# Sums of squares and reciprocal roots of the norms kept in PSUM banks

## The chip, the cores and the metric

The kernel runs on one core of one Trainium2 chip. The metric is the device time of one execution in microseconds (us), the median of several runs. A core has five engines that run side by side, each through its own list of instructions in order, with semaphores between them: PE (TensorE: matrix products into PSUM), DVE (VectorE), ACT (ScalarE), POOL (GpSimd) and SP (it issues transfers here). SBUF is the on-chip working memory, PSUM the accumulator memory of eight banks that PE writes and that DVE and ACT read and write.

## What is computed

One step of a two-layer transformer trunk over 640 tokens: 512 latent and 128 context tokens, width 1024, all in float32. In each layer: a norm with a modulation, an input projection, three attention branches with gates, an output projection, a second norm, a gated feed-forward part; one last norm at the end.

```python
def rmsnorm(x, g):
    xf = x.astype(jnp.float32)
    y = xf * lax.rsqrt(jnp.mean(xf * xf, axis=-1, keepdims=True) + EPS)
    return (y * g.astype(jnp.float32)).astype(x.dtype)

def trunk_layer(x, cvec, lp, mix_fn):
    sh1, sc1, g1, sh2, sc2, g2 = modulation(cvec, lp['w_mod'], lp['b_mod'])
    mixed, kv = mix_fn(rmsnorm(x, lp['norm1_g']) * (1.0 + sc1) + sh1)
    x = x + g1 * mixed
    x = x + g2 * swiglu(rmsnorm(x, lp['norm2_g']) * (1.0 + sc2) + sh2, lp['w_ffn_in'], lp['w_ffn_out'])
    return x, kv
```

## The kernel before

The state x lies transposed: eight tiles (`kt` or `m`, 0 to 7) of 128 channels by 640 tokens, each worked on in two halves of 320 tokens. A product of float32 precision is made of three passes with a high and a low part of each operand: `group` (lines 491 to 493) issues `wh·xh`, `wh·xl`, `wl·xh`. The low part of a weight tile, `wlo = raw - whi`, is made by POOL in one pass over 128x1024 (`lo`, line 457); in the attention part of the program some are made by an adding transfer instead.

A norm takes these steps, by half. `square_add` (lines 702 to 710), called as soon as a tile of x is final: ACT writes the square into an SBUF tile `sq`, DVE adds it to `ssq`. There is one `sq` buffer in the pool of line 1774 (two in the very first norm), so square and add of successive tiles take turns. When all eight are added, `rstd` (line 712) multiplies `ssq` by a matrix of ones on PE, into a PSUM bank of the kind `D`; ACT and DVE make the reciprocal root from it in four steps and leave it in the SBUF tile `ssq`. Then `norm` (line 731) goes through the eight tiles: DVE `nu = x * a * r` (line 749), ACT `h_hi = nu + b` (line 750), and for the low part either DVE `h_lo = (nu + b) - h_hi` (line 756) or, for tiles 2 and 5, ACT and POOL (lines 753 and 754). Each finished tile releases the matrix products that read it.

There are five norms: at the start; after the output projection of layer 0 (the second norm of layer 0, about 745 to 785 us); after its feed-forward part (the first norm of layer 1, about 1226 to 1260 us); after the output projection of layer 1 (its second norm, about 1929 to 1970 us); and the last one (about 2389 us to the end, `final`, line 1966). In the second norms the products `x2 = xr + g * d` are made from the bank `d` of the output projection by `residual` (line 1515), called in `out_proj` (line 1523); in the first norm of layer 1 and the last one by `ffn_out` (line 1729).

PSUM has four banks under the tag `B`, which the kinds `D` and `T` share, and four more for scores or, in the feed-forward part, under the tag `F`. There, two `D` banks and the four `F` banks go round as one list (`bank`, `bank_done`).

The order of the instructions on each engine is fixed when the program is built: `_Order` runs the tasks against a list of costs and priorities and writes the instructions down in the order in which they would start. DVE carries, beside the norms, the modulation of the layer (`mod_dve`, line 565, the rows `md`), and the small constants of the next attention (`attention_setup`, line 1932, the rows `lams` and `nlam`).

Of the kernel before, what the change touches and what calls it, by code (L numbers as in the profile page):

```python
# [26 lines left out]
AF = mybir.ActivationFunctionType  # L27
ALU = mybir.AluOpType
# [4 lines left out]
D = 1024  # L33
# [224 lines left out]
class _Trunk:  # L258
# [440 lines left out]

    def square_add(self, x, half, ssq, first):
        s = slice(half * HALF, (half + 1) * HALF)
        if first:
            yield self.act(ssq, x[:, s], AF.Square)
        else:
            q = yield from self.get("sq", [P, HALF])
            yield self.act(q, x[:, s], AF.Square)
            yield self.tt(ssq, ssq, q, ALU.add)
            self.rel("sq")  # L710

    def rstd(self, ssq):

        nc = self.nc
        d = yield from self.get("D", [P, 512])
        d = d[:, 0:HALF]
        yield self.pe(4 * HALF / 2400, lambda: nc.tensor.matmul(d, lhsT=self.ones, rhs=ssq, start=True, stop=True))
        u = yield from self.get("nu", [P, HALF])
        v = yield from self.get("nv", [P, HALF])
        yield self.act(u, d, AF.Ln, scale=1.0 / D, bias=self.eps)  # L720
        yield self.ts(v, d, 1.0 / D, EPS, ALU.mult, ALU.add)
        self.rel("D")
        yield self.act(ssq, u, AF.Exp, scale=-0.5)
        yield self.tt(u, ssq, ssq, ALU.mult)
        yield self.stt(u, u, -0.5, v, ALU.mult, ALU.mult)
        yield self.stt(ssq, u, 1.5, ssq, ALU.add, ALU.mult)
        self.rel("nu")
        self.rel("nv")
        return ssq

    def norm(self, l, which, x, half, ssq, h, ready, done):

        r = yield from self.rstd(ssq)
        left = [KT]

        def one(kt):
            yield self.wait(self.mod_ok[l][(0 if which == 0 else 12) + kt // 2])
            yield self.wait(self.mod_ok[l][(4 if which == 0 else 16) + kt // 2])
            a = self.acol[l][:, 8 * which + kt, :]
            sh = self.modc[l][:, (0 if which == 0 else 24) + kt, :]  # L740
            u = yield from self.get("nu", [P, HALF])
            o = half * HALF
            parts = []
            for s0, s1, c in self.segs(half):
                w = slice(s0 - o, s1 - o)
                b, hi = sh[:, c:c + 1], h[kt][:, 0, s0:s1]
                v = u[:, w]
                ops = [
                    self.stt(v, x[kt][:, s0:s1], a[:, c:c + 1], r[:, w], ALU.mult, ALU.mult),
                    self.act(hi, v, AF.Identity, bias=b),  # L750
                ]
                if kt in (POOL_FIRST if l == which == 0 else POOL_KT):
                    ops.append(self.act(v, v, AF.Identity, bias=b))
                    ops.append(self.ptt(h[kt][:, 1, s0:s1], v, hi.bitcast(F32), ALU.subtract))
                else:
                    ops.append(self.stt(h[kt][:, 1, s0:s1], v, b, hi.bitcast(F32), ALU.add, ALU.subtract))
                parts.append(ops)
            for ops in zip(*parts):
                yield self.both(*ops)
            self.rel("nu")  # L760
            self.o.fire(ready[kt])
            left[0] -= 1
            if left[0] == 0:
                self.rel("ssq")
                self.o.fire(done)

        for kt in range(KT):
            self.o.spawn(one(kt), 8 + half + 0.1 * kt)
# [754 lines left out]
    def out_proj(self, l, order, x2, ssq, ssq_ok):  # L1523
        src = self.I["x"] if l == 0 else self.xs
        hits = [self.counter(KT, lambda half=half: self.o.fire(ssq_ok[half])) for half in range(2)]
        ws, seen = {}, {m: 0 for m in range(KT)}
        xr, xr_ok = {}, {t: self.ev() for t in order}
        mg = self.merged
        first = [True, True]
        for m in range(KT):  # L1530
            x2[m] = self.t("x", [P, T])

        def load():
            for m, half in order:
                t = xr[m, half] = yield from self.get("xr", [P, HALF])
                yield self.dma(t, src[m][:, half * HALF:(half + 1) * HALF], 128 * 4 * HALF)
                self.o.fire(xr_ok[m, half])

        self.o.spawn(load(), 22)
        for m, half in order:  # L1540
            if m not in ws:
                ws[m] = yield from self.chunk()
            d = (yield from self.get("D", [P, 512]))[:, 0:HALF]
            yield from self.product(
                d, self.tiles(ws[m]), [lambda k=k: mg[k]["o"] for k in range(KT)], half,
                [mg[k]["half"][half] for k in range(KT)],
            )
            seen[m] += 1
            if seen[m] == 2:
                self.chunk_done()  # L1550

            def after(m=m, half=half, d=d, first_=first[half]):
                yield self.wait(xr_ok[m, half])
                for j in (8, 9, 10, 11):
                    yield self.wait(self.mod_ok[l][j])
                yield from self.residual(x2[m], xr[m, half], d, half, self.g1h[l][:, m, :])
                self.rel("D")
                self.rel("xr")
                if first_ and half == 0:
                    self.o.spawn(self.preload(), 8)  # L1560
                yield from self.square_add(x2[m], half, ssq[half], first_)
                hits[half]()

            first[half] = False
            self.o.spawn(after(), 7)
        for _ in range(KT):
            self.rel("u")
# [161 lines left out]
    def ffn_out(self, l, part, act, act_ok, x, ssq, ssq_ok, save):  # L1729

        end = part[-1] == NF - 1
        hits = [self.counter(KT, lambda half=half: self.o.fire(ssq_ok[half])) for half in range(2)]
        cur = {}
        n = len(part)

        def after(m, half, d):
            yield self.wait(self.mod_ok[l][20 + m // 2])
            xh = x[m][:, half * HALF:(half + 1) * HALF]
            yield from self.residual(x[m], xh, d, half, self.modc[l][:, 40 + m, :])
            self.bank_done(d)  # L1740
            if not end:
                return
            if m == half == 0:
                self.o.spawn(self.preload(), 8)
            yield from self.square_add(x[m], half, ssq[half], m == 0)
            hits[half]()
            if save and half == 1:
                yield self.dma(self.xs[m], x[m], 128 * 4 * T)

        split = (FO_SPLIT if end else KT) * n  # L1750
        steps = [(i // n, i % n, half) for i in range(split) for half in range(2)]
        steps += [(i // n, i % n, half) for half in range(2) for i in range(split, KT * n)]
        ds = {}
        for m, j, half in steps:
            if (m, half) not in ds:
                ds[m, half] = yield from self.bank()
            i, k = m * n + j, part[j]
            if i // 8 not in cur:
                cur[i // 8] = yield from self.chunk()
            wh, wl = (a[:, (i % 8) * P:(i % 8) * P + P] for a in cur[i // 8])  # L1760
            yield self.wait(act_ok[k])
            a, d = act[k], ds[m, half]
            yield self.group(d, wh, wl, a[:, 0, half], a[:, 1, half], j == 0, j == n - 1)
            if half == 1 and (i % 8 == 7 or i == KT * n - 1):
                self.chunk_done()
            if half == 1 and m == KT - 1:
                self.rel("act")
            if j == n - 1:
                self.o.spawn(after(m, half, d), 7)
# [463 lines left out]
```

## Time and profile before

| what | us |
|---|---|
| median of 3 runs | 2412.13 (2408.89 to 2419.16) |
| the profiled execution | 2411.09 |
| its span, first to last instruction | 2409.3 |
| PE busy | 2314.3 (96%) |
| DVE busy | 1771.2 (74%) |
| ACT busy | 1273.9 (53%) |
| POOL busy | 914.1 (38%) |

The profile is of one execution, with times from the start of its span. In its rows `L749` is a line of the kernel, though most operations are recorded by helpers and carry the helper's line: L336 is an activation of ACT, L359 and L363 are operations of DVE on two tensors, L375 one of POOL. `h<-nu,mo,h` says that h is written from nu, mo and h; `B`, `S` and `F` are PSUM banks, all other names stand for SBUF tiles or, on a transfer, for DRAM. "Idle before" is the time in which the engine had nothing running ahead of a row, and the name behind the arrow is what released it. The granted clock of PE is given as a share: 1.00 is 2.4 GHz, and it has one lower level, 1.2 GHz.

### The profile page before, as it was taken

What the parts mean: (1) busy time and instruction counts of PE and PEld (TensorE: products, weight loads), DVE (VectorE), ACT (ScalarE), POOL (GpSimd) and SP (SyncE); (2) the same over time, 40 slices, a digit from 0 to 9 for tenths busy, and PEclk for the clock granted to TensorE, in tenths of its full rate; (3) what the DMA queues carried; (4) which work ended last, traced back from release to release, by engine and by line L of the source; (5) the groups of instructions that cost most, each with busy time, mean ns of one, the idle gap of its engine ahead of it and who ended that gap; (6) DMA issues with size and microseconds to landing.
All of it is one profiled execution on the core that took longest, in us unless ns stands there. A gap on an engine that the chain in (4) does not pass through costs nothing.

```text
span 2409.3 us, 44479 instructions
## 1 busy us (share of the span) xinstructions
PE 2314.3 (96%) x16628; PEld 2265.0 (94%) x16628; DVE 1771.2 (74%) x4151; ACT 1273.9 (53%) x2818; POOL 914.1 (38%) x770
## 2 busy tenths in 40 slices
PE   7999899999998999999999999999999999999997
PEld 4999899999998999999889998999999989999997
DVE  7577788668489998999765778887672499666375
ACT  5677677667434432422457776777664254234143
POOL 3533411322123454645523425112221335456372
PEclk9999999999999999999989999999999999999998
DMA  6234332433774355453245444224436423322222
GB/s 252 75 94 115 77 85 59 108 88 88 207 233 151 107 164 172 135 171 128 95 135 123 99 111 98 72 64 101 107 85 145 133 100 114 106 71 85 74 76 74
DMA packets 100583, 275.79 MB, mean 114 GB/s; under 512 B 11408, under 2 KB 25360, under 8 KB 100368
## 3 DMA queue, kind: packets, MB, share of 16 engines
q1 hardware_dynamic: 84528, 215.28, 26.9%
q0 software_dynamic: 15840, 57.68, 12.5%
q8 instruction: 131, 2.15, 0.4%
q14 instruction: 84, 0.69, 0.1%
HBM read 208.43 MB, written 6.82 MB: 89 GB/s over the span
## 4 chain that ended last, share of the span: by engine, by line
PE 63%; DVE 13%; issue 7%; POOL 4%; DMA 3%; ACT 3%; DVEq 0%; POOLq 0%; SPq 0%; ACTq 0%
PE B L491 9%; PE B L492 8%; PE B L493 8%; PE F L493 6%; PE F L492 6%; PE F L491 5%; PE B L1127 4%; PE B L821 2%; PE B L823 2%; PE B L822 2%; PE S L1099 2%; POOL wlo L375 2%; PE S L1098 2%; PE B L1363 2%; PE B L1362 2%
## 5 line engine op out<-in xcount | busy, mean ns | idle before, releaser
L375 POOL TENSOR_TENSOR wlo<-raw,whi 128x1024 fp32r<-128x1024 f32 x158 | 391.9, 2486 | 350.5 <-ACT whi L336 340.4
L336 ACT ACTIVATE whi<-raw 128x1024 fp32r<-128x1024 f32 x268 | 282.9, 1055 | 257.7 <-PE F L492 89.7
L491 PE MATMUL B<-h,whi 128*128 128x320 f32 x972 | 308.2, 317 | 0.3 <-DVE acc L363 0.3
L493 PE MATMUL B<-h,wlo 128*128 128x320 f32 x972 | 301.0, 310 | 0.2 <-DMA wlo<-raw 0.2
L492 PE MATMUL B<-h,whi 128*128 128x320 f32 x972 | 300.6, 309 | 0.0
L821 PE MATMUL B<-whi,h 128*128 128x256 f32 x928 | 276.0, 297 | 1.8 <-ACT nat L336 1.2
L823 PE MATMUL B<-whi,h 128*128 128x256 f32 x928 | 264.6, 285 | 2.8 <-POOL h L375 2.5
L822 PE MATMUL B<-wlo,h 128*128 128x256 f32 x928 | 264.0, 284 | 0.0
L382 POOL DMA_DIRECT2D wlo<-raw x110 | 98.9, 899 | 323.9 <-ACT wlo L336 78.9
L336 ACT ACTIVATE P<-S,mx 128x768 f32<-128x768 f32 (+4 forms) x240 | 180.9, 756 | 54.6 <-DVE mx L1112 42.2
L491 PE MATMUL B<-u,whi 128*128 128x320 f32 x640 | 202.2, 316 | 0.4 <-DVE u L363 0.4
L375 POOL TENSOR_TENSOR wlo<-ws,whi 128x1024 fp32r<-128x1024 f32 x76 | 143.0, 1881 | 156.8 <-ACT whi L336 147.8
L493 PE MATMUL B<-u,wlo 128*128 128x320 f32 x640 | 198.3, 310 | 4.2 <-DMA wlo<-raw 4.2
L1112 DVE TENSOR_REDUCE mx<-S 128x1 f32<-128x768 f32 (+4 forms) x240 | 182.0, 765 | 22.7 <-PE S L1099 20.1
L492 PE MATMUL B<-u,whi 128*128 128x320 f32 x640 | 198.0, 309 | 0.0
L491 PEld LDWEIGHTS B<-h,whi 128*128 128x128 f32 x972 | 183.3, 189 | 1.3 <-DVE acc L363 0.6
L493 PEld LDWEIGHTS B<-h,wlo 128*128 128x128 f32 x972 | 182.9, 188 | 0.7 <-DMA wlo<-raw 0.7
L492 PEld LDWEIGHTS B<-h,whi 128*128 128x128 f32 x972 | 183.4, 189 | 0.0
L823 PEld LDWEIGHTS B<-whi,h 128*128 128x128 f32 x928 | 178.7, 193 | 3.9 <-POOL h L375 3.1
L821 PEld LDWEIGHTS B<-whi,h 128*128 128x128 f32 x928 | 179.0, 193 | 3.3 <-ACT nat L336 1.9
L822 PEld LDWEIGHTS B<-wlo,h 128*128 128x128 f32 x928 | 179.5, 193 | 0.0
L359 DVE TENSOR_TENSOR PT<-B,PT 128x512 fp32r<-128x512 f32 (+2 forms) x264 | 155.1, 608 | 32.5 <-ACT PT L336 30.5
(212 smaller groups left out, 7338.7 us busy)
## 6 DMA issues: line engine op xcount, KB each, us to landing
raw<-w SPq DMA_DIRECT2D x268, 512.0 KB, 3.4
wlo<-raw POOLq DMA_DIRECT2D x110, 512.0 KB, 4.7
mr<-wt SPq DMA_DIRECT2D x160, 256.0 KB, 3.2
u<-wm SPq DMA_DIRECT2D x12, 512.0 KB, 8.9
cr<-cb SPq DMA_DIRECT2D x14, 256.0 KB, 4.5
x<-x SPq DMA_DIRECT2D x8, 320.0 KB, 7.5
xr<-x SPq DMA_DIRECT2D x16, 160.0 KB, 3.5
xm<-x SPq DMA_DIRECT2D x8, 320.0 KB, 4.2
```

The source lines that it names most:

```text
L336: fn = lambda: self.nc.scalar.activation(out, in_, func, **kw)
L359: return self.dve(_n(out), lambda: self.nc.vector.tensor_tensor(out, a, b, op=op))
L375: return ("POOL", 0.147 + 0.0021 * _n(out), lambda: self.nc.gpsimd.tensor_tensor(out, a, b, op=op), 0.08)
L382: return ("POOL", 1.0, lambda: self.nc.gpsimd.dma_start(out=out, in_=in_, accum_op=ALU.add), 4.5)
L491: mm(out, lhsT=wh, rhs=xh, start=first, stop=False)
L492: mm(out, lhsT=wh, rhs=xl, start=False, stop=False)
L493: mm(out, lhsT=wl, rhs=xh, start=False, stop=last)
L821: mm(d, lhsT=hh, rhs=wh, start=kt == 0, stop=False)
L822: mm(d, lhsT=hh, rhs=wl, start=False, stop=False)
L823: mm(d, lhsT=hl, rhs=wh, start=False, stop=kt == KT - 1)
L1112: yield self.dve(w, lambda: nc.vector.tensor_reduce(m, s[:, 0:w], axis=AX.X, op=ALU.max, negate=True))
L1127: nc.tensor.transpose(t[:, i * P:(i + 1) * P], a, self.ident)
```

## The change

In the second norms of both layers, the first norm of layer 1 and the last norm, the square of a tile is written into the PSUM bank from which that tile of x was just made, and that bank is given back after the add and no more before the square. In the second norms and the first norm of layer 1, the reciprocal root is written over the product with ones in its PSUM bank, the eight `nu` products read it there, and the bank is given back after the eighth tile of the half. The first norm of layer 0 is as before; in the last norm the reciprocal root stays in SBUF.

```diff
-    def square_add(self, x, half, ssq, first):
+    def square_add(self, x, half, ssq, first, bank=None):
+
         s = slice(half * HALF, (half + 1) * HALF)
         if first:
             yield self.act(ssq, x[:, s], AF.Square)
+        elif bank is not None:
+            yield self.act(bank, x[:, s], AF.Square)
+            yield self.tt(ssq, ssq, bank, ALU.add)
         else:
...
-    def rstd(self, ssq):
+    def rstd(self, ssq, stay=False):
...
-        self.rel("D")
+        if not stay:
+            self.rel("D")
...
-        yield self.stt(ssq, u, 1.5, ssq, ALU.add, ALU.mult)
+        r = d if stay else ssq
+        yield self.stt(r, u, 1.5, ssq, ALU.add, ALU.mult)
...
-        return ssq
+        return r
...
-        r = yield from self.rstd(ssq)
+        stay = l > 0 or which > 0
+        r = yield from self.rstd(ssq, stay)
...
                 self.rel("ssq")
+                if stay:
+                    self.rel("D")
                 self.o.fire(done)
...
-                self.rel("D")
                 self.rel("xr")
                 if first_ and half == 0:
                     self.o.spawn(self.preload(), 8)
-                yield from self.square_add(x2[m], half, ssq[half], first_)
+                yield from self.square_add(x2[m], half, ssq[half], first_, d)
+                self.rel("D")
                 hits[half]()
...
-            self.bank_done(d)
             if not end:
+                self.bank_done(d)
                 return
             if m == half == 0:
                 self.o.spawn(self.preload(), 8)
-            yield from self.square_add(x[m], half, ssq[half], m == 0)
+            yield from self.square_add(x[m], half, ssq[half], m == 0, d)
+            self.bank_done(d)
             hits[half]()
```

On PE and POOL the order of the instructions is the same as before; on DVE, ACT and SP a few rows move. The first place is on DVE in the second norm of layer 0, where the reciprocal root of half 0 is finished while the last tiles of half 1 come in (x is the state, ac and mo the modulation, xr the old state, the numbers tell buffers apart). Before:

```order
L363 SCALAR_TENSOR_TENSOR ssq_8598<-nu_10107,ssq_8598 128x320
L363 SCALAR_TENSOR_TENSOR x_9569<-B_10115,gh_90,xr_10001 128x192
L363 SCALAR_TENSOR_TENSOR x_9569<-B_10115,gh_90,xr_10001 128x128
L363 SCALAR_TENSOR_TENSOR nu_10163<-x_9564,ac_89,ssq_8598 128x320
L363 SCALAR_TENSOR_TENSOR nu_10164<-x_9565,ac_89,ssq_8598 128x320
L359 TENSOR_TENSOR ssq_8599<-ssq_8599,sq_10173 128x320
L363 SCALAR_TENSOR_TENSOR h_10090<-nu_10163,mo_88,h_10090 128x320
```

And with the change:

```order
L363 SCALAR_TENSOR_TENSOR B_10088<-nu_10097,ssq_8598 128x320
L363 SCALAR_TENSOR_TENSOR x_9569<-B_10105,gh_90,xr_9994 128x192
L363 SCALAR_TENSOR_TENSOR x_9569<-B_10105,gh_90,xr_9994 128x128
L363 SCALAR_TENSOR_TENSOR nu_10152<-x_9564,ac_89,B_10088 128x320
L363 SCALAR_TENSOR_TENSOR nu_10153<-x_9565,ac_89,B_10088 128x320
L359 TENSOR_TENSOR ssq_8599<-ssq_8599,B_10105 128x320
L363 SCALAR_TENSOR_TENSOR h_10080<-nu_10152,mo_88,h_10080 128x320
```

The rows stand in the same order; the root, the `nu` products and the adds now name a bank, and the rows `h<-nu,mo,h` still name two SBUF tensors. It is the same in the second norm of layer 1.

The second place is on DVE in the first norm of layer 1, behind the row that reads the product with ones of half 1. Before:

```order
L371 TENSOR_SCALAR nv_15083<-B_15072 128x320
L359 TENSOR_TENSOR nat_15074<-nat_15070 128x128
L1955 TENSOR_REDUCE lams_15054<-nat_15074 128x2
L363 SCALAR_TENSOR_TENSOR h_14987<-nu_15086,mo_92,h_14987 128x320
L359 TENSOR_TENSOR nu_15082<-ssq_10487 128x320
```

And with the change:

```order
L371 TENSOR_SCALAR nv_15050<-B_15041 128x320
L363 SCALAR_TENSOR_TENSOR h_14961<-nu_15054,mo_92,h_14961 128x320
L359 TENSOR_TENSOR nu_15049<-ssq_10473 128x320
L363 SCALAR_TENSOR_TENSOR nu_15074<-x_9568,ac_93,B_14966 128x320
L363 SCALAR_TENSOR_TENSOR nu_15049<-nu_15049,nv_15050 128x320
```

The two small rows of the attention's constants (`nat`, `lams`) have gone behind the half's last `nu` products, so that the `h` row stands two rows further ahead. On SP, ahead of this norm, the load of one weight tile has gone behind the first store of the state (`xm<-x`), and the loads of three tables of constants for the next attention (rope, sm, lam) behind the last one.

## Rows read from the trace of the kernel before

**Rows 1.** The page, its first part: busy time, share of the span, instructions.

```profile
PE 2314.3 (96%) x16628; PEld 2265.0 (94%) x16628; DVE 1771.2 (74%) x4151; ACT 1273.9 (53%) x2818; POOL 914.1 (38%) x770
```

**Rows 2.** Windows around three norms: length, busy time by engine, PE clock, transfers.

```profile
core 0: us, PE busy (x) PEld busy (x) DVE busy (x) ACT busy (x) POOL busy (x), PEclk, DMA share, GB/s
...
750.00:768.00 18.00, 12.84 (x81) 11.95 (x79) 18.00 (x30) 8.58 (x16) 10.95 (x5) 0.93 0.25 87
...
1230.00:1245.00 15.00, 9.31 (x34) 7.34 (x34) 14.82 (x35) 10.11 (x21) 3.25 (x4) 0.60 0.78 204
...
1930.00:1950.00 20.00, 16.62 (x102) 15.44 (x101) 18.59 (x29) 11.28 (x20) 9.62 (x6) 0.91 0.23 79
1950.00:1970.00 20.00, 18.82 (x110) 18.05 (x109) 17.19 (x41) 11.49 (x29) 6.19 (x5) 0.83 0.31 102
```

**Rows 3.** Waits of PE, 745 to 770 us: total us, times, longest.

```profile
PE F L492 <- POOL h L375: 2.7, 1, 2.7
PE B L717 <- DVE ssq L359: 2.5, 2, 1.9
```

**Rows 4.** Waits of PE, 1225 to 1248 us.

```profile
PE B L823 <- POOL h L375: 2.5, 2, 1.8
```

**Rows 5.** Waits of PE, 1930 to 1958 us.

```profile
PE F L492 <- DVE h L363: 2.9, 1, 2.9
PE B L717 <- DVE ssq L359: 1.2, 1, 1.2
```

**Rows 6.** Timeline of DVE, second norm of layer 0: start, us, row, rows merged.

```profile
757.13 1.00 DVE L363 SCALAR_TENSOR_TENSOR nu<-x,ac,ssq 128x320 f32<-128x320 f32 x2
...
759.84 0.67 DVE L363 SCALAR_TENSOR_TENSOR x<-B,gh,xr 128x192 f32<-128x192 f32 x2
760.43 2.53 DVE L363 SCALAR_TENSOR_TENSOR nu<-x,ac,ssq 128x320 f32<-128x320 f32 x2
...
764.89 3.11 DVE L363 SCALAR_TENSOR_TENSOR nu<-x,ac,ssq 128x320 f32<-128x320 f32 x2
```

**Rows 7.** Timeline of POOL, the same stretch.

```profile
759.76 2.39 POOL L375 TENSOR_TENSOR wlo<-raw,whi 128x1024 fp32r<-128x1024 f32 x1 [3.56 <-ACT whi L336]
...
765.02 2.63 POOL L375 TENSOR_TENSOR wlo<-raw,whi 128x1024 fp32r<-128x1024 f32 x1 [0.40 <-ACT whi L336]
```

**Rows 8.** Groups of DVE over the whole span: count, busy us, mean ns, idle before.

```profile
L359 DVE TENSOR_TENSOR F<-F,s 128x320 f32<-128x320 f32 x60 | 29.1, 492 | 2.1 <-ACT s L336 1.5
L363 DVE SCALAR_TENSOR_TENSOR x<-F,mo,x 128x320 f32<-128x320 f32 x30 | 16.5, 550 | 60.9 <-PE F L493 60.9
```

**Rows 9.** Groups of ACT, 700 to 800 us.

```profile
L336 ACT ACTIVATE sq<-x 128x320 f32<-128x320 f32 x14 | 6.6, 468 | 27.2 <-DVE x L363 24.7 <-DVE ma L359 2.4
...
L336 ACT ACTIVATE B<-cr 128x512 f32<-128x512 f32 x2 | 1.2, 589 | 0.0
```

**Rows 10.** Timeline of DVE, second norm of layer 1.

```profile
1935.89 0.48 DVE L359 TENSOR_TENSOR ssq<-ssq,sq 128x320 f32<-128x320 f32 x1
...
1938.27 3.16 DVE L363 SCALAR_TENSOR_TENSOR nu<-x,ac,ssq 128x320 f32<-128x320 f32 x2
...
1941.75 1.00 DVE L363 SCALAR_TENSOR_TENSOR h<-nu,mo,h 128x320 fp32r<-128x320 f32 x2
...
1943.26 3.60 DVE L363 SCALAR_TENSOR_TENSOR nu<-x,ac,ssq 128x320 f32<-128x320 f32 x3
...
1947.19 0.54 DVE L363 SCALAR_TENSOR_TENSOR h<-nu,mo,h 128x320 fp32r<-128x320 f32 x1
...
1950.26 2.39 DVE L359 TENSOR_TENSOR ssq<-ssq,sq 128x320 f32<-128x320 f32 x1 [0.39 <-ACT sq L336]
```

**Rows 11.** Timeline of POOL, the same stretch.

```profile
1938.47 2.61 POOL L375 TENSOR_TENSOR wlo<-raw,whi 128x1024 fp32r<-128x1024 f32 x1 [3.36 <-ACT whi L336]
1942.55 0.93 POOL L375 TENSOR_TENSOR h<-nu,h 128x320 fp32r<-128x320 f32 x1 [1.48 <-ACT nu L336]
1943.50 2.56 POOL L375 TENSOR_TENSOR wlo<-raw,whi 128x1024 fp32r<-128x1024 f32 x1
```

**Rows 12.** Timeline of DVE, first norm of layer 1.

```profile
1235.79 1.96 DVE L363 SCALAR_TENSOR_TENSOR h<-nu,mo,h 128x320 fp32r<-128x320 f32 x1
```

**Rows 13.** Instructions of line 491, 1895 to 1945 us: duration ns, first and last start.

```profile
L491 PE MATMUL F<-h,whi x5: 305/309/411, 1942.0 to 1944.5; 128*128 128x320 f32 x5
```

**Rows 14.** Timeline of SP's queue, 1200 to 1260 us.

```profile
1205.49 9.51 SPq L378 DMA_DIRECT2D xm<-x  x3
...
1231.15 0.33 SPq L378 DMA_DIRECT2D xm<-x  x1
```

## The prediction

> **What bounds the kernel now.** I read the page first. PE is busy for 2314.3 of the span's 2409.3 us [rows 1], so what a norm can give back is time in which PE stands still, or runs at its lower clock, around a norm. The windows come next: they show PE busy for 12.84 of 18 us in the second norm of layer 0 (call it A), for 9.31 of 15 in the first norm of layer 1 (B), for 16.62 of 20 and 18.82 of 20 in the second norm of layer 1 (C) [rows 2]. PE is thus idle for 5.16 + 5.69 + 3.38 + 1.18 = 15.4 us in the three. DVE is busy for 18.00 of 18 in A, 14.82 of 15 in B and 18.59 of 20 in C: there it is the engine that is behind. The waits of PE say the same: it waits for the low part `h` or for `ssq`, products of DVE or of POOL behind DVE [rows 3 to 5].
>
> The granted clock falls in the same stretches, to means of 0.93, 0.60, 0.91 and 0.83 [rows 2]. At a lower level of 0.50 the time at half clock is (1 − mean) · 2 · length: 2.5 us in A, 12.0 in B, 3.6 + 6.8 = 10.4 in C. PE does half the work there, so these cost at most 1.25, 6.0 and 5.2 us.
>
> The third view is DVE's timeline beside POOL's. In A a pair of `nu` products takes 1.00 us at 757.13, but 2.53 at 760.43 and 3.11 at 764.89 [rows 6]. Both slow pairs lie over a POOL pass that makes a `wlo` tile: 759.76 for 2.39, 765.02 for 2.63 [rows 7]. Inside the first of these passes, at 759.84, DVE reads a bank, one tensor in SBUF and a small column (`x<-B,gh,xr`) and takes 0.67 for two rows [rows 6], so it isn't slowed. I read this as: a DVE row with two large SBUF inputs stands until POOL's pass ends, and a row with one of its inputs in PSUM doesn't. C repeats it: pair 3.16, trio 3.60, one add 2.39 [rows 10], with passes at 1938.47 and 1943.50 [rows 11].
>
> **What the change does, term by term.** It turns two of the rows that stand into rows with one SBUF input: `nu<-x,ac,ssq` (now with the bank for `ssq`) and `ssq<-ssq,sq` (now with the bank for `sq`). The rows of `h` and the squaring of the root keep two SBUF inputs. So a wait taken off a `nu` row may come back at the next `h` row, and each term has a low end for that.
>
> A. The two pairs lose 2.53 − 1.00 = 1.53 and 3.11 − 1.00 = 2.11 [rows 6]. If the next `h` takes over each wait, nothing is gained; if none does, 3.64. The order puts one add, now free to run, between the pair and its `h`, so a part is kept: I take the middle, **1.8**, range 0 to 3.6.
>
> B. `h` at 1235.79 takes 1.96 [rows 12], against 0.54 for a free one [rows 10]: 1.4 lost. Its inputs don't change, but two small rows leave the place ahead of it, so it may start before what holds it up. I take half, **0.7**, range 0 to 1.4. PE's 2.5 us behind POOL's `h` [rows 4] may hide it, which is the low end.
>
> C. The chain here is worked in order. The pair at 1938.27 is free, but the `h` pair behind it must stand until the pass ends at 1938.47 + 2.61 = 1941.08; it began at 1941.75, so 0.67 is kept. The trio at 1943.26 would take some 1.5 instead of 3.60, so 2.1 more. Its `h` at 1947.19 could start near 1944.4. POOL's second pass would be in its way: but POOL's own `h` before that pass [rows 11] waits for an ACT row behind the same `nu` rows, and can start at 1941.08 instead of 1942.55, which puts the pass at about 1942.0 to 1944.6. The `h` then starts near 1944.6, 2.6 earlier, and PE's 2.9 us of waiting for that row [rows 5] shrinks to 0.3. Last, the add at 1950.26 loses 2.39 − 0.48 = 1.9, and PE's product with ones waits for it. Sum 2.6 + 1.9 = **4.5**. Low end: the second pass stays where it was, to 1946.06, so that `h` gains 1.13, and with 1.9 that is 3.0. High end: every wait goes, 2.16 + 2.1 + 1.9 = 6.2.
>
> Clock. Less idle time should keep some of the lower clock away. Nothing at B, where most idle stays; at A and C 1.25 + 5.2 = 6.4 is the most. I take **1.5**, about a quarter, as about half of their 9.7 us of idle goes, and not all of that need lift the clock; range 0 to 3, and the whole of it is a rival.
>
> What I cost at nothing: ACT's square into a bank, since a 512-wide row into a bank takes 589 ns and a 320-wide square into SBUF 468 [rows 9], so the bank shows no surcharge; bounds ±0.1 us on each, and only a few are last in a chain. DVE with a bank as an operand: `x<-F,mo,x` takes 550 ns, `F<-F,s` 492 [rows 8], beside 0.54 for `h` [rows 10] and 0.48 for an add [rows 10]; at most 0.01 each. The last norm: its adds change, its `nu` rows don't, ±0.5. On SP, the weight load that goes behind the first of three stores (issued from 1205.49) is displaced by one issue, and the tables go behind the store at 1231.15 [rows 14] for an attention that starts after the norm; both lie beside PE's products. If that cover failed, a few tenths of a us for the load, and a wait of the next attention's DVE rows for the tables. The longer hold of the banks is priced as a rival.
>
> **Sum.** 1.8 + 0.7 + 4.5 + 1.5 = 8.5 us. The sum is made against the profiled execution, 2411.1 (span 2409.3): 2402.6. That execution lies 1.0 below the median of the three runs, 2412.1, so the forecast for a median is between 2402.6 and 2403.6: I say **2403**. Ends of the parts: 0 + 0 + 3.0 + 0 = 3.0, and 3.6 + 1.4 + 6.2 + 3 = 14.2, so this case's own range is 2397 to 2409.
>
> By these rows a PSUM operand costs nothing. The Trainium skill, page "Perfetto Trace Analysis", section "Optimizing Scalar/DVE Operations", gives DVE about 60 ns of access time on SBUF and about 125 ns on PSUM. The rows just named don't show these 65 ns; by the page the sum would be some 2 us smaller (worked out below).
>
> **Rivals.**
> - *The wait only moves.* The next `h`, or the squaring of the root, inherits each wait. For it: those rows still have two SBUF inputs. Against it: the add at C has no `h` behind it, and the passes end while free rows still run. Gain 1.9 (that add) plus about 0.7 (the `h` pair at C): some 2409.5. Chance 0.14.
> - *All waits go and the clock holds.* 3.6 + 1.4 + 6.2 + 6.4 = 17.6, so 2393.5 to 2394.5. Against it: `h` rows under a pass, and B's idle time, which is most of the clock's loss and barely moves. Chance 0.12 for over 14.2.
> - *A bank is dearer to read or write.* Some 36 DVE rows of this kind lie one behind the other on the three paths (eight `nu`, a root and seven adds of the half that comes last, three norms, less those under other work). The most that rows allow is 550 ns for `x<-F,mo,x` [rows 8] against half of the free pair of `nu`, 0.50 [rows 6]: 36 · 0.05 = 1.8 us less gain, 2404.8. Against it: one `h` without a bank takes 0.54 too. Chance 0.05. By the figure of the Trainium skill's page "Perfetto Trace Analysis" the estimate would be 36 · 0.065 = 2.3 us.
> - *Slower: the output projection of C runs out of banks.* Of four banks one is held by the root for eight `nu` rows, and each product's bank is now kept through the square and the add. The last product of half 1 ends when PE goes to `F<-h,whi` at 1942.0 [rows 13] and has 24 matmuls (eight tiles, three passes) of 16.62 / 102 = 0.16 each [rows 2], 3.9 in all, so it starts near 1938.1. It needs the bank whose add is now the row at 1935.89, which ends at 1936.4 [rows 10]: 1.7 us to spare. It decides from the point where that add comes more than 1.7 us later, as when one more POOL pass (2.6) stands over the DVE rows ahead of it. Then PE stands for up to 2.9 at C and a few tenths at A, the clock falls for as much again (2.9), and the gains are lost: 2411.1 + 6 = about 2417. Against it: the change makes DVE earlier, not later, and at 1935.89 no long row is near. Chance 0.04.
> - *It doesn't do what it says.* The order shows banks in the rows, so 0.01.
>
> The forecast keeps 0.64.
>
> **How the numbers follow.** 2395 to 2410 takes in the forecast's range and the first rival; outside lie half of the second rival, the fourth and a rest of the first, about 0.15. Half a per cent of 2412.1, about what a measurement of this kernel can tell from no change, is 12.1: faster means under 2400.1. Of the forecast, whose middle is 8.5, some 0.15 lies beyond 12.1; with all of the second rival that is 0.27. Slower, over 2424.2, would take the bank rival at more than twice its price: 0.02. The rest, 0.71, is within.
>
> **What would show it.** In the profile after, pairs of `nu<-x,ac,B` at 1.0 us under POOL's passes, and adds `ssq<-ssq,B` at 0.5, would show the mechanism right; pairs at 2.5 to 3 would show it wrong. `h` rows of 2 us or more, starting earlier, would show the first rival. PE's idle time should fall from 5.2 to about 3.4 at A, and from 4.6 to well under 2 at C; the mean clock in C should rise above 0.91 and 0.83. A wait of PE for `ssq` or an ACT square inside the output projection, at a `B<-u,whi` row, would show the banks. The forecast is wrong if free rows only let POOL's passes or the next engine (ACT's `h`, the weights' `whi`) become late by as much.

## The result and the profile after

The changed kernel takes 2399.01 us (median of 7 runs, 2396.04 to 2405.32) beside 2414.66 of the kernel before, measured with it (7 runs): a ratio of 0.9941, with a 95% interval of 0.9928 to 0.9954. It is faster by 0.6%, some 14 us. The profiled execution has a span of 2394.3 us, 15.0 less than the one read before. That is the forecast's direction, and the time lies within its range of 2397 to 2409. The gain is larger than that makes it look: the range was made from a median of 2412.13, and the kernel before came out at 2414.66 when it was measured again, so a gain of 14 to 15 lies at or just beyond the upper end of the forecast's 3.0 to 14.2 us.

All kernels of this study have PE's matmuls in one and the same order, so the n-th matmul of one trace is the n-th of another, and the span can be cut at the same work in both. The stages here are cut at PE's matmuls 5300 (737.0 us in the trace before), 6000 (856.4), 8300 (1216.7), 8600 (1267.0), 13500 (1915.1), 14200 (2035.4) and 16500 (2374.5); a number is the time between their starts. The last column runs from matmul 16500 to the start of the last one, the product with ones of the last norm.

| us | A: second norm, layer 0 | feed-forward, layer 0 | B: first norm, layer 1 | C: second norm, layer 1 | feed-forward, layer 1 | end, to the last matmul |
|---|---|---|---|---|---|---|
| before | 119.40 | 360.31 | 50.34 | 120.28 | 339.10 | 23.01 |
| after | 112.56 | 359.90 | 48.19 | 114.45 | 339.18 | 22.10 |
| difference | -6.84 | -0.41 | -2.15 | -5.83 | +0.08 | -0.91 |

The gain lies where it was looked for. What is not in the table is small: up to matmul 5300 the changed kernel takes 0.4 less, between 8600 and 13500 it takes 0.9 more, and from the start of the last matmul to the end of the span 12.30 instead of 11.84, so that 0.45 is left of the last column's 0.91.

The windows of the changed kernel, over the work of the four windows in [rows 2] to within five matmuls (length; busy time of PE, PE's loads, DVE, ACT, POOL; granted clock; transfers):

```profile
749.35:761.80 12.45, 11.61 (x78) 11.09 (x77) 12.45 (x30) 8.28 (x16) 9.63 (x5) 1.00 0.36 126
1222.90:1236.35 13.45, 9.15 (x35) 7.41 (x36) 13.15 (x32) 9.79 (x21) 2.63 (x3) 0.62 0.83 187
1921.65:1938.50 16.85, 15.59 (x102) 14.78 (x101) 15.95 (x29) 10.80 (x20) 9.40 (x6) 1.00 0.26 93
1938.50:1955.25 16.75, 16.44 (x111) 16.01 (x110) 14.75 (x41) 11.26 (x29) 4.45 (x5) 1.00 0.40 123
```

Two things are to be seen. PE's idle time fell from 5.16 to 0.84 in A, from 5.69 to 4.30 in B and from 4.56 to 1.26 + 0.31 = 1.57 in C. And the granted clock, 0.93, 0.91 and 0.83 before, is 1.00 in A and C; in B it stayed low, 0.62 after 0.60.

What the clock is worth is read from the stages of the table, which hold the same matmuls in both traces. A, B and C, before:

```profile
736.98:856.38 119.40, 109.29 (x703) 106.67 (x702) 115.83 (x230) 55.27 (x102) 52.22 (x27) 0.94 0.36 119
1216.69:1267.03 50.34, 44.65 (x302) 42.52 (x301) 33.91 (x84) 32.64 (x78) 17.83 (x26) 0.86 0.46 124
1915.08:2035.37 120.29, 110.54 (x703) 108.03 (x701) 105.46 (x187) 52.69 (x98) 51.90 (x26) 0.93 0.32 108
```

and after:

```profile
736.62:849.18 112.56, 106.45 (x703) 104.75 (x701) 109.44 (x229) 54.60 (x102) 52.05 (x27) 0.97 0.37 126
1209.08:1257.27 48.19, 43.67 (x302) 41.50 (x301) 32.10 (x84) 32.04 (x78) 16.78 (x26) 0.89 0.50 131
1906.23:2020.68 114.45, 107.39 (x702) 105.49 (x701) 98.33 (x187) 52.07 (x98) 50.24 (x26) 0.97 0.34 113
```

PE's idle time (length less busy time) fell by 4.0, 1.2 and 2.7 us, and its busy time for the same matmuls by 2.8, 1.0 and 3.1: nearly half of the gain is the higher clock.

DVE's timeline of A after, beside [rows 6]:

```profile
749.52 0.48 DVE L359 TENSOR_TENSOR ssq<-ssq,B 128x320 f32<-128x320 f32 x1
749.92 1.87 DVE L359 TENSOR_TENSOR nu<-ssq 128x320 f32<-128x320 f32 x1
...
752.23 0.15 DVE L359 TENSOR_TENSOR mo<-ma,sm 128x4 f32<-128x4 f32 x1
...
756.88 0.99 DVE L363 SCALAR_TENSOR_TENSOR nu<-x,ac,B 128x320 f32<-128x320 f32 x2
...
760.29 0.99 DVE L363 SCALAR_TENSOR_TENSOR nu<-x,ac,B 128x320 f32<-128x320 f32 x2
761.21 0.47 DVE L359 TENSOR_TENSOR ssq<-ssq,B 128x320 f32<-128x320 f32 x1
...
762.07 2.11 DVE L363 SCALAR_TENSOR_TENSOR h<-nu,mo,h 128x320 fp32r<-128x320 f32 x2
```

and POOL's, beside [rows 7]:

```profile
756.00 2.42 POOL L375 TENSOR_TENSOR wlo<-raw,whi 128x1024 fp32r<-128x1024 f32 x1 [0.89 <-ACT whi L336]
...
760.37 2.40 POOL L375 TENSOR_TENSOR wlo<-raw,whi 128x1024 fp32r<-128x1024 f32 x1 [0.34 <-ACT whi L336]
```

Both pairs of `nu` that took 2.53 and 3.11 now take 0.99, and they lie over POOL's passes as before. The last row shows what is left: an `h` pair, which still has two SBUF inputs, takes 2.11 (it began in the second of these passes, which ends at 762.77). The squaring of the root (749.92, 1.87) has taken over most of the wait of the add ahead of it, which took 2.28 before. And one small row was not in my working: before, the row `mo<-ma,sm` of the modulation, 128x4, stood under a pass too.

```profile
750.72 2.28 DVE L359 TENSOR_TENSOR ssq<-ssq,sq 128x320 f32<-128x320 f32 x1
...
753.85 2.37 DVE L359 TENSOR_TENSOR mo<-ma,sm 128x4 f32<-128x4 f32 x1
```

With the change it runs at 752.23 in 0.15, because DVE reaches it just before a pass (which starts at 752.48) instead of just behind the start of one (753.68 before): 2.2 us that come from a small shift. In C, DVE's timeline and then POOL's, beside [rows 10, 11]:

```profile
1929.40 1.00 DVE L363 SCALAR_TENSOR_TENSOR nu<-x,ac,B 128x320 f32<-128x320 f32 x2
...
1930.72 2.74 DVE L363 SCALAR_TENSOR_TENSOR h<-nu,mo,h 128x320 fp32r<-128x320 f32 x2
...
1933.96 1.45 DVE L363 SCALAR_TENSOR_TENSOR nu<-x,ac,B 128x320 f32<-128x320 f32 x3
...
1938.76 0.49 DVE L359 TENSOR_TENSOR ssq<-ssq,B 128x320 f32<-128x320 f32 x1 [0.40 <-ACT B L336]
```

```profile
1929.61 2.42 POOL L375 TENSOR_TENSOR wlo<-raw,whi 128x1024 fp32r<-128x1024 f32 x1 [3.36 <-ACT whi L336]
1931.98 1.13 POOL L375 TENSOR_TENSOR h<-nu,h 128x320 fp32r<-128x320 f32 x1
1933.07 2.64 POOL L375 TENSOR_TENSOR wlo<-raw,whi 128x1024 fp32r<-128x1024 f32 x1
```

The chain is the one that was worked out: the pair, the trio and the add are free (1.00, 1.45, 0.49 for 3.16, 3.60, 2.39), the `h` pair stands, and POOL's own `h` follows the first pass at once. PE's longest wait for that `h` fell from 2.9 [rows 5] to:

```profile
PE F L492 <- DVE h L363: 0.8, 1, 0.8
```

### The profile page after: what moved, and what is told of

The parts are those of the page before. It is cut to its first block, busy times and chain, and to the rows that moved or that the text cites. A ratio compares the mean times of both kernels' runs of the same rounds, so it can differ in the third digit from the quotient of the medians.

```text
span 2394.3 us, 44449 instructions
## 1 busy us (share of the span) xinstructions
PE 2305.8 (96%) x16628; PEld 2259.2 (94%) x16628; DVE 1748.7 (73%) x4151; ACT 1272.2 (53%) x2818; POOL 913.4 (38%) x770
## 3 DMA queue, kind: packets, MB, share of 16 engines
q8 instruction: 131, 2.15, 0.4%
## 4 chain that ended last, share of the span: by engine, by line
PE 62%; DVE 17%; issue 5%; POOL 3%; ACT 2%; DMA 2%; DVEq 0%; SPq 0%; POOLq 0%; ACTq 0%
PE B L491 9%; PE B L493 9%; PE B L492 9%; PE F L493 5%; PE F L492 5%; PE F L491 5%; PE B L1136 4%; PE B L830 3%; PE B L832 3%; PE B L831 3%; DVE md L617 2%; PE S L1108 2%; PE S L1107 2%; DVE act L359 2%; PE B L1372 2%
```

## The experiments

Theory P says that a DVE row with two SBUF inputs stands while a POOL instruction runs, and that the gain is that of rows with a bank in place of one input. Its rivals: the bank is a further buffer for squares (S), the gain comes from the few rows that moved (O), holding banks costs (H). Where no other kernel is named, an edit is against the changed kernel.

**Order and holds without the bank operands.** Bank holds and DVE's order are those of the change; squares go to `sq`, the root to `ssq`:

```diff
-            yield self.act(bank, x[:, s], AF.Square)
-            yield self.tt(ssq, ssq, bank, ALU.add)
+            q = yield from self.get("sq", [P, HALF])
+            yield self.act(q, x[:, s], AF.Square)
+            yield self.tt(ssq, ssq, q, ALU.add)
+            self.rel("sq")
...
-        r = d if stay else ssq
+        r = ssq
```

> Banks held and DVE's rows ordered exactly as in the change, but the squares go to the SBUF tile sq and the root to the SBUF tile ssq, so that every nu and ssq row keeps two SBUF inputs. Theory P (rows with two SBUF inputs stand under POOL's passes, and the gain is theirs alone): no gain beyond about 1 us, where the small rows of the constants moved, so 2411 to 2416 beside 2414.7 of before, and nu pairs of 2.5 to 3 us under the passes. Theory O (the gain comes from the moved rows): about 2400. Theory H (holding banks costs): over 2417, with PE waits at B<-u,whi rows.

2414.97, a ratio of 0.9998 (0.9986 to 1.0009): nothing gained and nothing lost, to within some 3 us. In C the pair and the pass stand as they did before:

```profile
1940.31 3.16 DVE L363 SCALAR_TENSOR_TENSOR nu<-x,ac,ssq 128x320 f32<-128x320 f32 x2
```

```profile
1940.51 2.61 POOL L375 TENSOR_TENSOR wlo<-raw,whi 128x1024 fp32r<-128x1024 f32 x1 [3.36 <-ACT whi L336]
```

This excludes O for the rows of DVE, and H as well: the banks are held as in the change, and PE's waits in C are the same 2.9 and 1.2 as in [rows 5]. (On SP the load of one weight tile stands here as in the kernel before; the run with the squares alone, below, has the change's order on every engine.)

**Two buffers for the squares** in the kernel before.

```diff
-    def open_x(self, sq=1):
+    def open_x(self, sq=2):
```

> The kernel before with two sq buffers in place of one in every norm, so that the square of a tile need not wait for the add of the one before; nothing else. Theory S (the bank helps as a further buffer for squares): most of the gain, 2400 to 2404. Theory P: no change, within 2 us of before, since ACT's squares wait for x rows and not for sq.

2413.99, 0.9993 (0.9983 to 1.0002). No gain that can be told, so S falls: the interval leaves at most 4 us of the 14.

**The change in two halves.** Only the root in its bank (the squares, and the release of the product's bank, as before):

```diff
+                self.rel("D")
...
-                yield from self.square_add(x2[m], half, ssq[half], first_, d)
-                self.rel("D")
+                yield from self.square_add(x2[m], half, ssq[half], first_)
...
+            self.bank_done(d)
             if not end:
-                self.bank_done(d)
...
-            yield from self.square_add(x[m], half, ssq[half], m == 0, d)
-            self.bank_done(d)
+            yield from self.square_add(x[m], half, ssq[half], m == 0)
```

> Only the reciprocal root stays in its bank (nu reads it there); squares and their banks as before. Theory P: the nu rows run free but the adds stand: in the second norm of layer 0 about 3.5 us (the two pairs; the add at 750.7 still stands and the small mo row behind it too), in the first norm of layer 1 about 0.6, in the second norm of layer 1 2.6 to 4, with a little of the clock: 2405 to 2408. Theory S: no gain.

2410.37, 0.9982 (0.9972 to 0.9992): about 4 us, less than expected. Only the squares in their banks:

```diff
-        stay = l > 0 or which > 0
+        stay = False
```

> Only the squares go into the banks; the root is copied to SBUF as before. Theory P: the adds run free and the nu rows stand: about 2.6 us in the second norm of layer 0 (0.4 at the add, 2.2 at the small mo row that then slips ahead of the next pass), 1.9 in the second norm of layer 1, 0.7 at the last norm: 2408 to 2411. Theory S: the whole gain, about 2400.

2411.18, 0.999 (0.9981 to 0.9999): about 2.4 us, just outside what was expected. The order on every engine is that of the change here, so the moved rows are worth no more than that.

The halves sum to 7 us, the whole is 14 to 15. By stage, root alone gives 2.60 in A, 0.23 in B and 0.38 in C; squares alone 1.70, 0.02 and 2.52; the whole 6.84, 2.15 and 5.83. Why C gives the root so little is seen in its DVE timeline:

```profile
1933.90 1.00 DVE L363 SCALAR_TENSOR_TENSOR nu<-x,ac,B 128x320 f32<-128x320 f32 x2
1934.82 2.06 DVE L359 TENSOR_TENSOR ssq<-ssq,sq 128x320 f32<-128x320 f32 x1
1936.79 3.74 DVE L363 SCALAR_TENSOR_TENSOR h<-nu,mo,h 128x320 fp32r<-128x320 f32 x2
...
1945.87 2.39 DVE L359 TENSOR_TENSOR ssq<-ssq,sq 128x320 f32<-128x320 f32 x1 [0.43 <-ACT sq L336]
```

The freed pair takes 1.00, the add behind it stands for 2.06, and the `h` pair meets the next POOL rows and takes 3.74. That is the first rival of the prediction, and it is true of half the change: a wait that is taken off one row goes to the next row that can stand. Only with both kinds of row freed does DVE run through most of a pass.

**Shorter POOL instructions.** In the kernel before, the low-part passes of the output projection's and the first feed-forward tiles are cut into four, in the same place of POOL's order (`both` writes the four down one behind the other, and `g[1]` keeps the price of one whole pass, so that the order of the program doesn't change):

```diff
-                        yield self.ptt(c["lo"][n][:, 0:w], x, c["hi"][n][:, 0:w].bitcast(F32), ALU.subtract)
+                        g = self.ptt(c["lo"][n][:, 0:w], x, c["hi"][n][:, 0:w].bitcast(F32), ALU.subtract)
+                        if not c["seven"] and O_WO <= c["src"] < O_FI + 2 * PLAIN:
+                            q = [slice(i * w // 4, (i + 1) * w // 4) for i in range(4)]
+                            k = self.both(*(self.ptt(c["lo"][n][:, s], x[:, s], c["hi"][n][:, s].bitcast(F32), ALU.subtract) for s in q))
+                            g = (g[0], g[1], k[2], g[3])
+                        yield g
```

> The kernel before, with POOL's low-part passes of the output projection's and the first feed-forward tiles (the passes that lie over the two second norms) cut into four pieces of 256 columns, order and all else unchanged. Theory P (a row with two SBUF inputs stands until the POOL instruction that runs ends): it can start between pieces, so pairs of nu take 1.0 to 1.7 us instead of 2.5 to 3.2, and the program gains 5 to 12 us, 2403 to 2410. If the rows stood for another reason than POOL's instruction (the bank, ACT, the source tile): no change, 2412 to 2417.

2409.17, 0.9975 (0.9961 to 0.9988), a gain of 6 us with no bank operand at all. The 12 runs lie far apart, 2400.78 to 2417.48, and the profiled one took 2416.30: its rows show the mechanism, not the gain. In C, DVE and then POOL:

```profile
1946.56 1.49 DVE L363 SCALAR_TENSOR_TENSOR nu<-x,ac,ssq 128x320 f32<-128x320 f32 x2
...
1951.40 2.46 DVE L363 SCALAR_TENSOR_TENSOR nu<-x,ac,ssq 128x320 f32<-128x320 f32 x3
```

```profile
1946.76 3.79 POOL L375 TENSOR_TENSOR wlo<-raw,whi 128x256 fp32r<-128x256 f32 x4 [1.97 <-ACT whi L336]
```

The same pair takes 1.49 instead of 3.16 and the trio 2.46 instead of 3.60, with nothing changed but the length of POOL's instructions; POOL pays, 3.79 for a tile instead of 2.61. So it is POOL's instruction that DVE's row waits for, and its end that lets it go. A gained 3.2 us by stage and C 3.3, which this execution lost again in the feed-forward part of layer 0 (see the next run). The Trainium skill, page "SBUF — State Buffer", section "Who interferes with whom", has this as a rule: a DVE instruction with two SBUF inputs contends with a GpSimd instruction that reads SBUF, and one with at most one SBUF input, outside DVE's two-port modes, doesn't. The pair's 1.00 us with a bank against 3.16 without, and 1.49 with short pieces, agree.

**The change with these pieces.**

> The changed kernel with the same four pieces. Theory P: the waits that the change left (h pairs of 2.1 and 2.7 us, the root's row of 2.7) shrink to under 1.6, 1 to 4 us less than the change, 2395 to 2399. The change's own gain over the kernel with pieces should shrink to 3 to 9 us. Otherwise: same as the change, 2399.

2405.6, 0.9956 (0.9942 to 0.997): not better than the change. A and C are shorter by 0.8 and 3.0 us than with the change alone (111.77 and 111.42), but the feed-forward part of layer 0 takes 369.09 instead of 359.90. The kernel with pieces and without the change shows the same there, 367.78. The instructions of that part are unchanged; only the time at which DVE and POOL enter it differs. So that part has waits of its own. That the time of entry decides how many DVE rows fall under a pass there is an inference; which rows they are was not followed up.

**Pieces in every pass from the output projection on**, the feed-forward parts included (the condition above becomes `c["seven"] or c["src"] >= O_WO`), with the change:

> The changed kernel with the pieces in every low-part pass from the output projection on, so all through the feed-forward parts too. Theory P: DVE rows of the feed-forward parts (act, ht, ws, 2 to 3 us where they stand) shorten, but POOL's passes lengthen as they take turns with DVE. DVE and POOL are both ahead of PE there, so little of it reaches the end: 2390 to 2399. If POOL becomes the late one: over 2402.

2370.55, 0.9809 (0.9795 to 0.9824): 46 us faster than before, far more than expected. The feed-forward part of layer 0 fell from 359.90 to 340.15, which is what the same part of layer 1 took all along (339.10): DVE carries the modulation of layer 1 there, and some of its rows stand under passes. The groups of DVE over the whole span, before:

```profile
L359 DVE TENSOR_TENSOR ws<-raw 128x512 f32<-128x512 f32 x38 | 86.9, 2286 | 11.3 <-POOL wlo L375 7.4 <-DMA raw<-w 3.8
...
L359 DVE TENSOR_TENSOR ma<-ma 128x4 f32<-128x4 f32 x40 | 28.7, 719 | 0.7
```

and with the change and the pieces:

```profile
L359 DVE TENSOR_TENSOR ws<-raw 128x512 f32<-128x512 f32 x38 | 42.4, 1115 | 21.3 <-POOL wlo L375 17.1 <-DMA raw<-w 3.9
...
L359 DVE TENSOR_TENSOR ma<-ma 128x4 f32<-128x4 f32 x40 | 14.4, 361 | 0.7
```

A row on four columns that takes 719 ns on average is a row that waits; another of that size took 0.15 us at 752.23. How these waits reach PE can be read from a stretch of 90 us in that part. Before (a window, and three waits in it: total us, times, longest):

```profile
985.00:1075.00 90.00, 82.64 (x538) 80.26 (x537) 87.59 (x190) 30.06 (x48) 49.46 (x22) 0.98 0.42 139
```

```profile
POOL wlo L375 <- ACT whi L336: 38.6, 13, 4.6
...
ACT whi L336 <- DVE ws L359: 9.0, 4, 4.1
...
PE F L493 <- POOL wlo L375: 5.1, 4, 1.6
```

and with the change and the pieces:

```profile
975.00:1065.00 90.00, 89.18 (x606) 88.64 (x605) 80.65 (x209) 30.50 (x49) 68.36 (x97) 1.00 0.50 168
```

Before, DVE is busy for 87.59 of the 90 us: it is the engine that is behind, and PE feels it through ACT's `whi` and POOL's `wlo`, which PE waits for. With the pieces DVE is busy for 80.65 while PE gets 606 matmuls done instead of 538. No run tests this path by itself.

**The same pieces without the change.**

> The kernel before with POOL's low-part passes cut into four from the output projection on (as in the run that came to 2370.6 with the change in it). It tells what the change is worth once no POOL instruction runs longer than about 0.9 us. Theory P: a row then stands for a third as long, so the change's own gain shrinks from 15 us to 5 to 12 (in the run with pieces over the second norms alone it was 2409.2 to 2405.6): 2376 to 2383. If the change's gain had nothing to do with the length of POOL's instructions: 15 us, so 2386.

2382.15, 0.9867 (0.985 to 0.9885), so the pieces alone give 32 us. The change is worth 11.6 us more by the medians, 14 by the ratios (0.9867 less 0.9809, each to its own measurement of the kernel before), and 13.3 by stage up to the last matmul: A 112.77 to 109.28, B 51.28 to 47.97, C 114.77 to 109.29, the end 23.09 to 22.10. I had expected 5 to 12, so its gain hardly shrank. In A the pieces take over half of what the change gives (3.5 for 6.8), in B and C nothing to speak of (3.3 and 5.5 for 2.2 and 5.8): shorter waits at rows on the path are still waits.

**Two pieces, and eight,** with the change:

> The change with two pieces (512 columns) instead of four. Theory P: the waits go with the length of the piece, so the gain of the pieces lies between none (2399) and four (2370.6), nearer to four since many rows stand only near the end of a pass: 2376 to 2388.

> The change with eight pieces (128 columns). Theory P: DVE's waits shrink once more, but POOL pays eight starts (about 0.2 us more each than its share of columns) and lets DVE in eight times, so POOL, which PE already waits for, becomes the late one in places: 2366 to 2378, no clear gain over four.

Two: 2379.82, 0.9855 (0.9838 to 0.9873), between none and four, as expected. Eight: 2461.41, 1.0195 (1.0177 to 1.0213), where I had POOL late in places, but no loss. POOL's groups with four and with eight, and PE's wait with eight:

```profile
L375 POOL TENSOR_TENSOR wlo<-raw,whi 128x256 fp32r<-128x256 f32 x592 | 474.5, 836 | 212.2 <-ACT whi L336 206.3 <-DMA raw<-w 4.2 <-PE B L498 1.4
```

```profile
L375 POOL TENSOR_TENSOR wlo<-raw,whi 128x128 fp32r<-128x128 f32 x1184 | 566.0, 518 | 185.5 <-ACT whi L336 185.5
```

```profile
PE F L498 <- POOL wlo L375: 27.1, 31, 1.6
```

A tile costs POOL 4 · 836 = 3.3 us in four and 8 · 518 = 4.1 in eight (2.5 whole). PE, which waited for `wlo` in F 1.4 us in all with four pieces, waits 27.1 with eight, and both feed-forward parts grow by about 40 us: 382.07 and 376.88. So it is POOL's `wlo` that PE now waits for.

**The root's own rows.** With the change, the first estimate of the root goes into the bank too, so that its steps have one SBUF input each:

```diff
-        yield self.act(ssq, u, AF.Exp, scale=-0.5)
-        yield self.tt(u, ssq, ssq, ALU.mult)
-        yield self.stt(u, u, -0.5, v, ALU.mult, ALU.mult)
         r = d if stay else ssq
-        yield self.stt(r, u, 1.5, ssq, ALU.add, ALU.mult)
+        yield self.act(r, u, AF.Exp, scale=-0.5)
+        yield self.stt(u, r, -0.5, v, ALU.mult, ALU.mult)
+        yield self.tt(u, u, r, ALU.mult)
+        yield self.stt(r, u, 1.5, r, ALU.add, ALU.mult)
```

> The changed kernel with the reciprocal root's steps rewritten so that the first estimate lies in the bank too and no step but the last norm's has two SBUF inputs (r times v, times r, in place of r squared times v). Theory P: the row that takes 2.69 us in the second norm of layer 1, half 0, takes 0.5, and about 1.5 to 2 us of that reaches PE unless the next h row inherits it; the estimate now waits for the row that reads the product, 0.5 us more in each norm. 2396 to 2400.

2399.51, 0.9932 (0.9917 to 0.9947), the same as the change. C gained 1.6 us (112.81), since its second step takes 0.49 where the old one took 2.69, but A took 2.4 more (114.95), B 1.0 more (49.21), and the feed-forward part of layer 0 came out at 364.18 in that execution (2402.93). Why A and B lost was not followed up. The step in C:

```profile
1932.31 0.49 DVE L359 TENSOR_TENSOR nu<-nu,B 128x320 f32<-128x320 f32 x1
```

**All together:** the change, these steps, and four pieces in every pass from the program's start.

> The change with the root's steps in the bank (as in the run of 2399.5), and four pieces in every low-part pass, the first ten tiles at the program's start included. At C the root's row is already shorter with pieces, so at most 1 us from the root; at the start a few rows of the first norm stand under passes, 0 to 4 us: 2365 to 2371.

2369.12, 0.981 (0.9792 to 0.9827). It is not to be told from the 2370.55 without the root's steps. Either is 1.9% faster than the kernel before, and 1.3% than the change (0.981 / 0.9941).

## Why the prediction was right, point by point

*The reading was right.* That a row with two SBUF inputs stands under POOL's passes and one with a bank doesn't was read from three slow pairs. The pieces show it by themselves, 6 us without a bank operand, and the control with banks held and rows moved, which gained nothing, leaves the operand as the cause of the change's gain.

*The terms.* Idle time and busy time of PE, from the stages of before and after:

| | forecast | measured | from |
|---|---|---|---|
| A | 1.8 (0 to 3.6) | 4.0 | idle 10.11 to 6.11 |
| B | 0.7 (0 to 1.4) | 1.2 | idle 5.69 to 4.52 |
| C | 4.5 (3.0 to 6.2) | 2.7 | idle 9.75 to 7.06 |
| clock | 1.5 (0 to 3) | 7.0 | busy time less 2.84, 0.98, 3.15 |
| last norm | 0 (-0.5 to 0.5) | 0.45 | 34.85 to 34.40 from matmul 16500 to the end of the span |
| sum | 8.5 | 15.3 | span: 15.0 |

Three terms lie outside their bounds, A and the clock above and C below. That the time still fell in the range is in part luck: the range was made of all the ends together, and the reference moved by 2.5 us. The largest miss is the **clock**: I took "about a quarter" of what lay there, on the ground that half the idle time would go. In the four windows 75% of it went in A and C, (9.72 - 2.41) / 9.72, and the clock stayed at 1.00 in them. What lay there was also more than the 6.4 us that I had given as the most: the window of A ended at 768, and the lower clock went on behind it,

```profile
768.00:785.00 17.00, 16.54 (x98) 15.73 (x99) 16.04 (x41) 11.66 (x29) 3.17 (x5) 0.88 0.36 109
```

and B, where I had put nothing, gave 1.0. What PE did before or while its clock fell in A and C was stand still for single waits of up to 2.9 us [rows 3, 5]; after, the longest is 1.2 in A and 0.8 in C. In B one wait of PE for `ssq` takes 2.3 before and after, and the clock falls behind it in both. The rival "all waits go and the clock holds" was nearer in this term than the forecast.

**A** was mis-sized because "the next `h` takes half" is a guess where a row could have been looked for. The `h` rows in A took over 0.3 (the pair at 754.65, 1.26) and 1.1 (the pair at 762.07), and the row `mo<-ma,sm`, which I hadn't listed among those that stand, gave 2.2 by a shift. A list of all rows with two SBUF inputs under a pass, small ones too, would have shown it.

In **B** the moved rows did what I had taken them for, and it was not enough: in the control, which has them, the `h` row takes 1.36 instead of 1.96, but the stage gains only 0.12 (squares alone, 0.02). The whole change gives 2.15, and one row that differs is POOL's. It takes 1.45 in the control, beside a `nu` pair from SBUF, and 0.87 with the change, beside one from the bank:

```profile
1241.33 1.45 POOL L375 TENSOR_TENSOR h<-nu,h 128x320 fp32r<-128x320 f32 x1 [3.36 <-ACT nu L336]
```

```profile
1232.31 0.87 POOL L375 TENSOR_TENSOR h<-nu,h 128x320 fp32r<-128x320 f32 x1 [3.35 <-ACT nu L336]
```

So POOL's row can be the one that is longer, too. PE's waits for POOL's `h` fell from 2.5 [rows 4] to 1.3, and to 1.9 in the control; the rest of B's gain is the clock, and why that rose sooner with the whole change, and neither in the control nor in the two halves, stays open.

In **C** the chain was right: its last add ended at 1950.26 + 2.39 = 1952.65 and now ends at 1938.76 + 0.49 = 1939.25, 13.4 earlier, of which PE's matmul 13500 had 8.9 already (1915.1 to 1906.2 us). That is the 4.5 worked out. The stage lost 5.8, but only 2.7 of it is idle time, and 3.1 is busy time: part of the wait that the chain took away had been filled with matmuls at the lower clock, and stands in the row of the clock.

The **last norm** gains because its last add, 1.15 under a POOL row at 2395.66, takes 0.47 at 2381.07. Of these 0.7 us, 0.2 go again at the five rows of the first half's result behind it, 2.60 instead of 2.39.

*Nothing for the bank.* The surcharge on a PSUM operand, a rival by a figure of the Trainium skill, page "Perfetto Trace Analysis", section "Optimizing Scalar/DVE Operations" (about 125 ns for DVE on PSUM, about 60 on SBUF), doesn't show here. ACT's square is even shorter into a bank, 438 ns for 467 over the whole span before:

```profile
L336 ACT ACTIVATE B<-x 128x320 f32<-128x320 f32 x38 | 16.7, 438 | 54.4 <-DVE x L363 54.4
```

and the add from a bank takes 485 ns, which a free add from SBUF took before [rows 10]:

```profile
L359 DVE TENSOR_TENSOR ssq<-ssq,B 128x320 f32<-128x320 f32 x38 | 18.4, 485 | 7.4 <-ACT B L336 7.4
```

That the same section gives ACT a shorter access on PSUM than on SBUF (about 51 ns and 93) agrees in its sign with the 29 ns between the two squares.

*The rivals.* Holding the banks costs nothing here (control: 0.9998). "The wait only moves" came true for each half alone, and for single rows of the whole. I gave 0.71 to a change within half a per cent; it came out at 0.59% (0.46 to 0.72), the case that had 0.27.

## What to carry to other kernels

Where two engines share a path, list every row of the one that can stand under a long instruction of the other, small rows included, and look at the pairs of start and end in both timelines: a 128x4 row of 2.4 us says more than a busy share of 74%. Freeing one kind of row hands the wait to the next one that can stand, so free them together, or shorten the instruction that they wait for: cutting POOL's 2.5 us passes into four was worth more (32 us) than the change (14 us), and eight pieces, with the change, came out 47 us slower than the kernel before, so the number has to be measured. And where the idle time in a stretch goes, count the lower clock that it brought as well.

## What was not expected

- The gains of the two halves (4.3 and 2.4 us by their ratios) are together half of the whole's.
- The feed-forward part of layer 0 takes 359.6 to 369.1 us with the same instructions, and 340.2 once POOL's passes are in four. PE's own waits hardly put these 20 us down to DVE: from 985 to 1075 us PE of the kernel before waits 6.5 us for POOL's `wlo` and 0.7 for DVE, though DVE is busy for 87.59 of these 90 us.
- Eight pieces make POOL's tile 24% dearer than four (4.1 for 3.3 us), and the program 90 us longer.
